# Laying out the model dimension as 512 a + 4 p + j in a two-layer trunk with a mixture of experts

## The chip, the cores and the metric

The kernel runs on one core of a Trainium2 chip. The metric is device time in microseconds (us), from the first to the last instruction of the program with what lies around them; lower is better. TensorE is called PE, its weight loads PEld, VectorE DVE, ScalarE ACT, GpSimd POOL and SyncE SP, as in the profile. MB is a million bytes, KB is 1024 bytes.

## What is computed

The reference is a trunk of two layers on 256 tokens of 1024 features, in 32-bit floats. Each layer has a mixer (layer 0: a convolution and a stick-breaking attention; layer 1: gated linear attention and pooling) and then a mixture of experts. The mixers are left out here; what the change is about is the second half of each layer, and it is mostly reading weights: 16 experts a layer with three matrices of 2 MB each.

```python
D_MODEL = 1024; SEQ = 256; DEPTH = 2; N_EXPERTS = 16; TOP_K = 2; D_EXPERT = 512
for l in range(DEPTH):
    mod = cond @ ada_w[l] + ada_b[l]                  # six vectors: shift, scale, gate, twice
    h = rmsnorm(x, norm_mix[l]) * (1 + sc1) + sh1
    x = x + g1 * mixer(h, w_in, w_out, ...)
    h = rmsnorm(x, norm_ffn[l]) * (1 + sc2) + sh2
    combine = weights of the two chosen experts of each token, zero elsewhere
    y = 0
    for e in range(N_EXPERTS):
        act = silu(h @ w_gate[l, e]) * (h @ w_up[l, e])      # 1024 -> 512
        y = y + combine[:, e] * (act @ w_down[l, e])         # 512 -> 1024
    x = x + g2 * y
return rmsnorm(x, final_norm)
```

## The kernel before, in words

**Layout.** A matrix with 1024 rows is used in eight blocks of 128 rows, one row on each partition. Which rows make a block is free, as long as the weights and the activations agree. `rows` (line 72) splits the row number as 256 a + 2 p + j, with a from 0 to 3, p the partition and j 0 or 1; block k is a = k // 2, j = k % 2, and `block` (line 76) picks it out of an array whose columns run over the features. In such a slice each element lies two elements behind the one before. It is read by PE as the matrix that is loaded into the array in the transposes of `vecs`, `xn` and `arow` (lines 129, 143, 197), in the output projection (line 451) and in the scatter of layer 0 (line 1323), and it is written as an output at line 1522.

**Units and the ring.** All large weights go through a ring of 16 buffers of 1 MB (8 KB a partition), `buffer` at line 50. A buffer's worth is called a unit here. Units are taken from the ring in the order in which the code asks for them, nearly all are loaded by DMAs that SP issues in that order, and a DMA waits on SP until the unit that lay in its buffer 16 units earlier has been read by its last matmul. `unit` (line 62) loads the projections' and the modulation's weights: `ada` with n = 2 (line 183) takes one row of 2048 columns on each partition, 8 KB in one piece; `Projections.load` (line 396) takes four rows of 512 columns, 2 KB each, in two DMAs.

**The experts.** They are worked off in eight pairs (`pr`), each expert with at most 64 tokens in the common case. `weight(pr, i)` (line 1206) loads unit i of a pair: 0 to 3 are `w_gate`, 4 to 7 `w_up`, 8 to 11 `w_down`. A unit holds a quarter of the rows of both experts of the pair: for `w_gate` and `w_up` the blocks 2i and 2i + 1, for `w_down` one block of 128 rows. On each partition that is 4 KB of one expert and 4 KB of the other. `up` (line 1231) takes a unit for every two blocks, and for each block one matmul of 512 columns for each expert; in the trace each such matmul is two instructions, so a unit is eight of them. `down` (line 1266) takes a unit for every block and does two halves of 512 columns for each expert. In names of tiles `w0_1_6` is layer 0, pair 1, unit 6; in the page the numbers are left out.

**Order.** The program is written out in its order by hand (`manual_schedule`). In layer 0, `up` of pair 0 has the gathers of the tokens between its blocks (`gathered`, line 1448, one gather of two blocks of `xg` for every two blocks of the matmul). From pair 1 on the order is gate, up, scatter of an earlier pair, down of the pair before, transposes of the activations. In pair 7 PE does the gate product, a scatter, a branch that skips code for experts with more than 64 tokens (`rest`, line 1369), the down product of pair 6, the up product of pair 7 in two halves with scatters, and the last down product. The mixers' projections take units of the same ring (`part`, line 398, splits a block of a unit into a high and a low half on ACT and DVE).

Of the kernel before, what the change touches and what calls it, by code (L numbers as in the profile page):

```python
# [16 lines left out]
D = 1024  # L17
# [12 lines left out]
def trunk(ctx: ExitStack, tc: tile.TileContext, x, c, ada_w, ada_b, norm_mix, norm_ffn,  # L30
# [31 lines left out]
    def unit(name, src, a, eng=SP):  # L62

        t = buffer(name).rearrange("p (a b) -> p a b", a=a)
        if len(src.shape) == 4:
            for i in range(2):
                eng.dma_start(t[:, 2 * i:2 * i + 2], src[:, i])
        else:
            eng.dma_start(t, src)
        return t  # L70

    def rows(w):

        return w.rearrange("(a p j) n -> p a j n", a=4, j=2)

    def block(ap, k):

        a, j = k // 2, k % 2
        return ap[:, 256 * a + j:256 * a + 256:2]
# [96 lines left out]
    def ada(l, s, n):  # L176
# [4 lines left out]
        for i in range(4 * n):  # L181
            if n == 2:
                w = unit(f"ad{nm_}{i}", src[:, i // 2, i % 2:i % 2 + 1, s * D:(s + 2) * D], 1)
            else:
                w = unit(f"ad{nm_}{i}", src[:, i, :, s * D:(s + 1) * D], 2)
# [44 lines left out]
    def small_loads():  # L230
        G.dma_start(rb, router_bias.rearrange("(o e) -> o e", o=1).broadcast_to([128, E]))
        for a in range(4):
            G.dma_start(rw[:, 2 * a:2 * a + 2], rows(router_w)[:, a])
        for a in range(4):
            G.dma_start(walow[:, 2 * a:2 * a + 2, 0:16], rows(w_in_odd[0])[:, a, :, 1536:1552])
# [151 lines left out]
    class Projections:  # L387
# [5 lines left out]
        def load(self, eng=SP):  # L393
            n, k = len(self.w) // 2, len(self.w) % 2 * 4
            c0 = self.firsts[n]
            self.w.append(unit(f"wi{c0}{k}", self.src[:, k // 2:k // 2 + 2, :, c0:c0 + 512], 4, eng))
# [723 lines left out]
    def moe(l, pool, nrm, psacc, after, following=None):  # L1120
# [85 lines left out]
        def weight(pr, i, out=None, eng=SP):  # L1206

            if i < 8:
                src = (moe_w_gate, moe_w_up)[i // 4][l, 2 * pr:2 * pr + 2]
                src = src.rearrange("e (a p j) n -> p a e (j n)", a=4, j=2)[:, i % 4]  # L1210
            else:
                src = moe_w_down[l, 2 * pr:2 * pr + 2, (i - 8) * 128:(i - 7) * 128].rearrange("e p n -> p e n")
            if out is None:
                out = buffer(f"w{l}_{pr}_{i}")
            if l and pr == 7 and i >= 10:

                out = out.rearrange("p (k e n) -> p k e n", k=2, e=2)
                for n in (last_parts[:1], last_parts[1:])[i - 10]:
                    for k in range(2):
                        src = moe_w_down[l, 14:16, (2 + k) * 128:(3 + k) * 128, n].rearrange("e p n -> p e n")  # L1220
                        SP.dma_start(out[:, k, :, within(n)], src)
                return out
            out = out.rearrange("p (e n) -> p e n", e=2)
            eng.dma_start(out, src)
            return out

# [4 lines left out]
        def up(pr, s, w, xg, name, between=None):  # L1231
            b = bank(f"{name}{l}_{pr}_{s}")
            o = 128 * (pr % 2)
            for k in range(8):
                if between:
                    between(k)
                if k % 2 == 0:
                    we = next(w)
                for e in range(2):
                    PE.matmul(b[64 * e:64 * e + 64, :], lhsT=xg[:, k, o + 64 * e:o + 64 * e + 64],  # L1240
                              rhs=we[:, e, k % 2 * 512:k % 2 * 512 + 512], start=k == 0, stop=k == 7)
            return b

        def act(pr, s, gb_, ub, sg=None):
# [8 lines left out]
            return a  # L1253
# [398 lines left out]
```

## Time and profile before

| | us |
|---|---|
| three runs: median (lowest, highest) | 797.86 (795.85, 861.59) |
| the profiled execution's own time | 801.36 |
| its span, first to last instruction | 799.6 |

The rows quoted below come from the profiled execution, all times in them from the start of its span. In a timeline a row gives the start, the time, the engine, the line, the operation, output and inputs, shapes and the count; a bracket at its end says how long the engine had been idle and what ended that. In the table by windows each engine's busy time is followed by its number of instructions, then come the granted PE clock (1.00 is 2.4 GHz), the mean busy share of the DMA engines and the rate in GB/s. A row "A <- B: t, n, m" of the waits says that A waited t us for B in n waits, the longest m.

### The profile page before, as it was taken

The numbers are of one execution on the slowest core, as the hardware profiler recorded it, in microseconds if no ns is written. First come the engines' busy times: TensorE is split into PE (matmuls) and PEld (weight loads), VectorE is DVE, ScalarE is ACT, GpSimd is POOL, SyncE is SP. The second block draws the span as 40 slices with busy tenths as digits, with TensorE's granted clock in tenths as the row PEclk, the third lists the DMA queues.
The fourth block names the chain that finished last, engine by engine and source line by source line (L and its number), as shares of the span: only waits on it lengthen the run. The fifth ranks groups of instructions, "written<-read, shape, count | busy, mean of one in ns | idle before, by whom it ended". The sixth has DMA issues, their size and how long they took to land. (4 is left out here: it accounts for less than half of the span.)

```text
span 799.6 us, 10666 instructions
## 1 busy us (share of the span) xinstructions
PE 736.6 (92%) x4177; PEld 404.3 (51%) x4177; DVE 314.4 (39%) x563; ACT 235.1 (29%) x441; POOL 118.9 (15%) x168
## 2 busy tenths in 40 slices
PE   7898798998999999999697999999699999999985
PEld 4498555586434344353233677578434334434323
DVE  4459968575213112130115655453513123213114
ACT  3357647463102001110113543551402001001012
POOL 2347646222000000000014500010200000000000
PEclk9999989999999999999989999999899999999988
DMA  9999739954999999999999997495799999999991
GB/s 358 385 376 419 267 120 394 372 224 192 351 412 409 409 409 409 410 408 409 407 401 389 401 413 247 182 390 204 292 362 411 410 409 409 410 410 409 408 381 58
DMA packets 74718, 282.52 MB, mean 353 GB/s; under 512 B 5194, under 2 KB 6438, under 8 KB 69530
## 3 DMA queue, kind: packets, MB, share of 16 engines
q1 hardware_dynamic: 73122, 278.68, 89.0%
q0 software_dynamic: 1344, 2.64, 0.9%
q8 instruction: 37, 0.61, 0.3%
q10 hardware_dynamic: 184, 0.34, 0.1%
q14 instruction: 31, 0.25, 0.1%
HBM read 280.59 MB, written 1.05 MB: 352 GB/s over the span
## 5 line engine op out<-in xcount | busy, mean ns | idle before, releaser
L1240 PE MATMUL g<-w,xg 128*64 128x512 f32 x512 | 115.9, 601 | 1.9 <-DMA w<-in_moe_w_gate_dram 1.8
L1273 PE MATMUL dn<-w,at 128*64 128x512 f32 x448 | 105.6, 623 | 11.5 <-PEq L1372 5.7
L1240 PE MATMUL u<-w,xg 128*64 128x512 f32 x496 | 110.6, 594 | 1.9 <-DMA w<-in_moe_w_up_dram 1.9
L1273 PEld LDWEIGHTS dn<-w,at 128*64 128x64 f32 x448 | 32.3, 143 | 77.0 <-issue 59.9
L1252 DVE TENSOR_TENSOR act<-sg,u 128x512 f32<-128x512 f32 (+1 forms) x18 | 11.1, 628 | 152.6 <-PE u L1240 152.6
L1240 PEld LDWEIGHTS u<-w,xg 128*64 128x64 f32 x496 | 34.7, 137 | 71.6 <-issue 64.7
L1240 PEld LDWEIGHTS g<-w,xg 128*64 128x64 f32 x512 | 35.3, 138 | 69.4 <-issue 62.9
L421 PE MATMUL pj<-hT,g 128*128 128x256 f32 x480 | 62.5, 288 | 7.0 <-DVE g L56 4.6
L56 DVE TENSOR_TENSOR g<-wi,g 128x512 fp32r<-128x512 f32 x72 | 58.2, 816 | 25.6 <-ACT g L55 24.5
L421 PEld LDWEIGHTS pj<-hT,g 128*128 128x128 f32 x480 | 59.2, 193 | 10.7 <-DVE g L56 6.7
L416 PE MATMUL pj<-g,hT 128*128 128x512 f32 x192 | 51.2, 414 | 7.5 <-DVE g L56 3.6
L55 ACT ACTIVATE g<-wi 128x512 fp32r<-128x512 f32 x72 | 44.4, 626 | 39.7 <-PE pj L421 20.9
L451 PE MATMUL po<-cat,g 128*128 128x256 f32 x372 | 51.1, 290 | 2.5 <-ACT gsr L994 1.7
L188 PE MATMUL ada<-ad,cond 128*32 128x512 f32 x384 | 50.6, 632 | 0.0
L451 PEld LDWEIGHTS po<-cat,g 128*128 128x128 f32 x372 | 46.8, 196 | 6.7 <-ACT gsr L994 2.6
L416 PEld LDWEIGHTS pj<-g,hT 128*128 128x128 f32 x192 | 35.6, 194 | 22.3 <-DVE g L56 6.7
L556 POOL TENSOR_TENSOR yc<-yc,cv 128x256 f32<-128x256 f32 x45 | 38.7, 860 | 24.3 <-ACT cv L555 21.6
L541 DVE SCALAR_TENSOR_TENSOR yc<-yp,epar,yc 128x256 f32<-128x256 f32 x56 | 41.2, 736 | 1.0
L1305 ACT ACTIVATE ys<-y 128x512 fp32r<-128x512 f32 x28 | 16.9, 625 | 70.4 <-DVE y L1295 50.2
L1263 DVE COPY at<-at 128x512 f32<-128x512 f32 x14 | 9.7, 692 | 68.0 <-PE at L1262 68.0
L1299 ACT ACTIVATE y<-dn,cw 128x512 f32<-128x512 f32 x7 | 4.8, 687 | 107.4 <-PE dn L1273 107.4
L1248 ACT ACTIVATE sg<-g 128x512 f32<-128x512 f32 x14 | 8.4, 597 | 89.4 <-PE g L1240 86.3
(385 smaller groups left out, 886.4 us busy)
## 6 DMA issues: line engine op xcount, KB each, us to landing
w<-in_moe_w_gate_dram SPq DMA_DIRECT2D x64, 1024.0 KB, 16.1
w<-in_moe_w_up_dram SPq DMA_DIRECT2D x62, 1024.0 KB, 18.4
w<-in_moe_w_down_dram SPq DMA_DIRECT2D x61, 1024.0 KB, 18.2
ad<-in_ada_w_dram SPq DMA_DIRECT2D x48, 1024.0 KB, 8.9
wi<-in_w_in_even_dram SPq DMA_DIRECT2D x20, 512.0 KB, 13.0
wi<-in_w_in_odd_dram SPq DMA_DIRECT2D x14, 512.0 KB, 12.6
wo<-in_w_out_even_dram SPq DMA_DIRECT2D x4, 1024.0 KB
wo<-in_w_out_odd_dram SPq DMA_DIRECT2D x4, 1024.0 KB, 16.6
```

The costliest lines, as they stand in the source:

```text
L55: S.activation(g[0], w, AF.Copy)
L56: (eng or V).tensor_tensor(g[1], w, g[0].bitcast(F32), op=OP.subtract)
L188: PE.matmul(acc[32 * j:32 * j + 32, :], lhsT=cond[:, k, :], rhs=w[:, k - (i if n == 2 else 2 * i), c0:c0 + 512], start=i == 0, stop=i == 4 ...
L416: PE.matmul(bs[t], lhsT=self.h[j][:, k, t * 128:(t + 1) * 128], rhs=g[i], start=k == 0 and p == 0, stop=k == 7 and p == 2)
L421: PE.matmul(bs[c // 2][:, (c % 2) * T:(c % 2 + 1) * T], lhsT=g[i][:, c * 128:(c + 1) * 128], rhs=self.h[j][:, k, :], start=k == 0 and c % ...
L451: PE.matmul(self.acc[kd // 2][:, (kd % 2) * T:(kd % 2 + 1) * T], lhsT=block(g[wi], kd % 4), rhs=cats[ci][:, k, :], start=start and kd % 2 ...
L541: V.scalar_tensor_tensor(yc[:, k], yp[:, k, j:j + T], epar[:, k, j:j + 1], yc[:, k], op0=OP.mult, op1=OP.add)
L556: G.tensor_tensor(y, y, p, op=OP.add)
L1240: PE.matmul(b[64 * e:64 * e + 64, :], lhsT=xg[:, k, o + 64 * e:o + 64 * e + 64], rhs=we[:, e, k % 2 * 512:k % 2 * 512 + 512], start=k == 0 ...
L1252: V.tensor_tensor(a[:, n], sg[:, n], ub[:, n], op=OP.mult)
L1273: PE.matmul(bs[h][64 * e:64 * e + 64, :], lhsT=at[k][:, 64 * e:64 * e + 64], rhs=r[:, e], start=k == 0, stop=k == 3)
L1305: S.activation(ys[:, 0, n], y[h], AF.Copy)
```

## The change

The row number is split as 512 a + 4 p + j, with a 0 or 1 and j from 0 to 3, so block k is a = k // 4, j = k % 4, and a slice of `block` has its elements four apart. A unit of an expert pair holds half the rows of one expert instead of a quarter of both: 8 KB of one expert in one piece on each partition. Even units belong to the pair's first expert, odd ones to the second. `up` takes two units for every four blocks, `down` takes two for every two. `w_down` is split in the same manner (`rows_down`, 256 a + 2 p + j), and so the transposes of the activations pick every other column. The projections' units are loaded by one DMA instead of two, with pieces of 2 KB as before; router weights and the small gate weights by two DMAs instead of four. The last units of layer 1 keep their size and shape. Left out of the diff are the same edits in `rest`.

```diff
--- before.py
+++ after.py
@@ -62,21 +62,17 @@
     def unit(name, src, a, eng=SP):
 
         t = buffer(name).rearrange("p (a b) -> p a b", a=a)
-        if len(src.shape) == 4:
-            for i in range(2):
-                eng.dma_start(t[:, 2 * i:2 * i + 2], src[:, i])
-        else:
-            eng.dma_start(t, src)
+        eng.dma_start(t, src)
         return t
 
     def rows(w):
 
-        return w.rearrange("(a p j) n -> p a j n", a=4, j=2)
+        return w.rearrange("(a p j) n -> p a j n", a=2, j=4)
 
     def block(ap, k):
 
-        a, j = k // 2, k % 2
-        return ap[:, 256 * a + j:256 * a + 256:2]
+        a, j = k // 4, k % 4
+        return ap[:, 512 * a + j:512 * a + 512:4]
 
     def halves(tile2):
         return tile2.rearrange("p (j t) -> p j t", j=2)
@@ -180,9 +176,9 @@
         src = rows(ada_w[l])
         for i in range(4 * n):
             if n == 2:
-                w = unit(f"ad{nm_}{i}", src[:, i // 2, i % 2:i % 2 + 1, s * D:(s + 2) * D], 1)
+                w = unit(f"ad{nm_}{i}", src[:, i // 4, i % 4:i % 4 + 1, s * D:(s + 2) * D], 1)
             else:
-                w = unit(f"ad{nm_}{i}", src[:, i, :, s * D:(s + 1) * D], 2)
+                w = unit(f"ad{nm_}{i}", src[:, i // 2, i % 2 * 2:i % 2 * 2 + 2, s * D:(s + 1) * D], 2)
             for j in range(4):
                 k, c0 = (i, j * 512) if n == 2 else (2 * i + j // 2, j % 2 * 512)
                 PE.matmul(acc[32 * j:32 * j + 32, :], lhsT=cond[:, k, :],
@@ -229,10 +225,10 @@
 
     def small_loads():
         G.dma_start(rb, router_bias.rearrange("(o e) -> o e", o=1).broadcast_to([128, E]))
-        for a in range(4):
-            G.dma_start(rw[:, 2 * a:2 * a + 2], rows(router_w)[:, a])
-        for a in range(4):
-            G.dma_start(walow[:, 2 * a:2 * a + 2, 0:16], rows(w_in_odd[0])[:, a, :, 1536:1552])
+        for a in range(2):
+            G.dma_start(rw[:, 4 * a:4 * a + 4], rows(router_w)[:, a])
+        for a in range(2):
+            G.dma_start(walow[:, 4 * a:4 * a + 4, 0:16], rows(w_in_odd[0])[:, a, :, 1536:1552])
         for j in range(4):
             G.dma_start(gw[32 * j:32 * j + 16], gla_gate_w[0])
 
@@ -393,7 +389,7 @@
         def load(self, eng=SP):
             n, k = len(self.w) // 2, len(self.w) % 2 * 4
             c0 = self.firsts[n]
-            self.w.append(unit(f"wi{c0}{k}", self.src[:, k // 2:k // 2 + 2, :, c0:c0 + 512], 4, eng))
+            self.w.append(unit(f"wi{c0}{k}", self.src[:, k // 4, :, c0:c0 + 512], 4, eng))
 
         def part(self):
             i = len(self.parts)
@@ -1205,24 +1201,27 @@
 
         def weight(pr, i, out=None, eng=SP):
 
+            e = 2 * pr + i % 2
             if i < 8:
-                src = (moe_w_gate, moe_w_up)[i // 4][l, 2 * pr:2 * pr + 2]
-                src = src.rearrange("e (a p j) n -> p a e (j n)", a=4, j=2)[:, i % 4]
+                src = rows((moe_w_gate, moe_w_up)[i // 4][l, e])[:, i // 2 % 2]
             else:
-                src = moe_w_down[l, 2 * pr:2 * pr + 2, (i - 8) * 128:(i - 7) * 128].rearrange("e p n -> p e n")
+                src = rows_down(e)[:, (i - 8) // 2]
             if out is None:
                 out = buffer(f"w{l}_{pr}_{i}")
             if l and pr == 7 and i >= 10:
 
                 out = out.rearrange("p (k e n) -> p k e n", k=2, e=2)
                 for n in (last_parts[:1], last_parts[1:])[i - 10]:
-                    for k in range(2):
-                        src = moe_w_down[l, 14:16, (2 + k) * 128:(3 + k) * 128, n].rearrange("e p n -> p e n")
-                        SP.dma_start(out[:, k, :, within(n)], src)
+                    for e in range(2):
+                        SP.dma_start(out[:, :, e, within(n)], rows_down(14 + e)[:, 1, :, n])
                 return out
-            out = out.rearrange("p (e n) -> p e n", e=2)
+            out = out.rearrange("p (j n) -> p j n", j=src.shape[1])
             eng.dma_start(out, src)
             return out
+
+        def rows_down(e):
+
+            return moe_w_down[l, e].rearrange("(a p j) n -> p a j n", a=2, j=2)
 
         def weights(pr, first, last):
             for i in range(first, last):
@@ -1234,11 +1233,11 @@
             for k in range(8):
                 if between:
                     between(k)
-                if k % 2 == 0:
-                    we = next(w)
+                if k % 4 == 0:
+                    we = [next(w), next(w)]
                 for e in range(2):
                     PE.matmul(b[64 * e:64 * e + 64, :], lhsT=xg[:, k, o + 64 * e:o + 64 * e + 64],
-                              rhs=we[:, e, k % 2 * 512:k % 2 * 512 + 512], start=k == 0, stop=k == 7)
+                              rhs=we[e][:, k % 4], start=k == 0, stop=k == 7)
             return b
 
         def act(pr, s, gb_, ub, sg=None):
@@ -1250,7 +1249,7 @@
             sg, ub = (b.rearrange("s (k p) -> s k p", k=4) for b in (sg, ub))
             for n in [slice(0, 4)] if pr < 7 else [slice(0, 2), slice(2, 4)]:
                 V.tensor_tensor(a[:, n], sg[:, n], ub[:, n], op=OP.mult)
-            return a
+            return a.rearrange("s k p -> s (k p)")
 
         def actT(pr, s, a, *at):
             nm_ = f"{l}_{pr}_{s}"
@@ -1259,7 +1258,8 @@
             at = [t.rearrange("p (k s) -> p k s", k=4)[:, 0:n] for t in at]
             for i, b in enumerate(bs):
                 for k in range(n):
-                    PE.transpose(b[:, k, :], a[:, i * n + k, :], ident)
+                    f = i * n + k
+                    PE.transpose(b[:, k, :], a[:, f // 2 * 256 + f % 2:f // 2 * 256 + 256:2], ident)
                 V.tensor_copy(at[i], b)
             return [t[:, k, :] for t in at for k in range(n)]
 
@@ -1270,19 +1270,20 @@
 
             def product(h, k, r):
                 for e in range(2):
-                    PE.matmul(bs[h][64 * e:64 * e + 64, :], lhsT=at[k][:, 64 * e:64 * e + 64], rhs=r[:, e],
+                    PE.matmul(bs[h][64 * e:64 * e + 64, :], lhsT=at[k][:, 64 * e:64 * e + 64], rhs=r[e],
                               start=k == 0, stop=k == 3)
 
-            for k in range(2 if l and pr == 7 else 4):
-                we = next(w)
-                for h, n in enumerate(cols):
-                    product(h, k, we[:, :, n])
+            for a in range(1 if l and pr == 7 else 2):
+                we = [next(w), next(w)]
+                for j in range(2):
+                    for h, n in enumerate(cols):
+                        product(h, 2 * a + j, [w_[:, j, n] for w_ in we])
             if l and pr == 7:
                 for h, n in enumerate(cols):
                     if h < 2:
                         we = next(w)
                     for k in range(2):
-                        product(h, 2 + k, we[:, k, :, within(n)])
+                        product(h, 2 + k, [we[:, k, e, within(n)] for e in range(2)])
             return bs
 
         def weighted(pr, s, bs, cw):
...
```

**Where instructions move.** On PE, in the gate product of pair 0 of layer 0 (`g0_0_0` is its output, `acc02` the bank of a gather between), before:

```order
L1240 MATMUL g0_0_0_1944<-w0_0_0_1955,xg0_0_1924 64x512 x4
L1175 MATMUL acc02_1920<-P0_0_1922,hn0h_1825 128x256 x2
L1175 MATMUL acc02_1920<-P0_0_1922,hn0l_1826 128x256 x2
L1175 MATMUL acc02_1920<-P0_0_1922,hn0h_1825 128x256 x2
L1175 MATMUL acc02_1920<-P0_0_1922,hn0l_1826 128x256 x2
L1240 MATMUL g0_0_0_1944<-w0_0_1_1971,xg0_0_1924 64x512 x4
```

And the same place of the changed kernel:

```order
L1239 MATMUL g0_0_0_1930<-w0_0_0_1941,xg0_0_1910 64x512
L1239 MATMUL g0_0_0_1930<-w0_0_1_1943,xg0_0_1910 64x512
...
L1171 MATMUL acc02_1906<-P0_0_1908,hn0h_1811 128x256 x2
L1171 MATMUL acc02_1906<-P0_0_1908,hn0l_1812 128x256 x2
L1171 MATMUL acc02_1906<-P0_0_1908,hn0h_1811 128x256 x2
L1171 MATMUL acc02_1906<-P0_0_1908,hn0l_1812 128x256 x2
L1239 MATMUL g0_0_0_1930<-w0_0_0_1941,xg0_0_1910 64x512
L1239 MATMUL g0_0_0_1930<-w0_0_1_1943,xg0_0_1910 64x512
```

Unit `w0_0_0` had been read to its end ahead of that gather; now its last matmul, and with it the point from which its buffer is free, stands behind the gather, beside that of `w0_0_1`.

On SP, the DMAs that stand 16 units behind those two, before (`w0_1_6` takes the buffer of `w0_0_0`, `w0_1_7` that of `w0_0_1`):

```order
L1224 DMA w0_1_5_2098<-in_moe_w_up_dram 128x2x1024
L1224 DMA w0_1_6_2104<-in_moe_w_up_dram 128x2x1024
L1224 DMA w0_1_7_2110<-in_moe_w_up_dram 128x2x1024
L1224 DMA w0_0_8_2129<-in_moe_w_down_dram 128x2x1024
L1224 DMA w0_0_9_2135<-in_moe_w_down_dram 128x2x1024
```

And of the changed kernel:

```order
L1219 DMA w0_1_5_2080<-in_moe_w_up_dram 128x2048
L1219 DMA w0_1_6_2090<-in_moe_w_up_dram 128x2048
L1219 DMA w0_1_7_2092<-in_moe_w_up_dram 128x2048
L1219 DMA w0_0_8_2115<-in_moe_w_down_dram 128x2048
L1219 DMA w0_0_9_2117<-in_moe_w_down_dram 128x2048
```

The order of the units on SP is what it was; each is now one run of 2048 elements on a partition instead of two of 1024.

## Rows read from the trace of the kernel before

**Rows 1.** The page: DMA packets, and DMA issues (KB each, us to landing).

```profile
DMA packets 74718, 282.52 MB, mean 353 GB/s; under 512 B 5194, under 2 KB 6438, under 8 KB 69530
...
w<-in_moe_w_gate_dram SPq DMA_DIRECT2D x64, 1024.0 KB, 16.1
...
ad<-in_ada_w_dram SPq DMA_DIRECT2D x48, 1024.0 KB, 8.9
```

**Rows 2.** Table by windows: PE, PEld, DVE, ACT, POOL busy, clock, DMA share, GB/s.

```profile
10.00:22.00 12.00, 12.00 (x59) 4.61 (x57) 5.72 (x9) 3.64 (x6) 5.23 (x8) 1.00 1.01 426
28.00:44.00 16.00, 12.77 (x86) 11.02 (x86) 11.65 (x21) 9.77 (x18) 7.54 (x8) 0.89 1.05 387
56.00:74.00 18.00, 15.99 (x129) 15.17 (x128) 16.41 (x22) 11.84 (x24) 11.07 (x12) 1.00 1.01 419
...
220.00:380.00 160.00, 156.40 (x802) 65.53 (x798) 32.68 (x54) 19.42 (x33) 0.00 (x0) 1.00 1.03 409
600.00:760.00 160.00, 157.80 (x782) 68.01 (x778) 38.52 (x63) 19.67 (x34) 0.00 (x0) 1.00 1.03 409
```

**Rows 3.** Waits of PE's weight loads, 200 to 410 us: those on DMAs.

```profile
PEld u L1240 <- DMA w<-in_moe_w_up_dram: 6.0, 5, 1.5
PEld dn L1273 <- DMA w<-in_moe_w_down_dram: 5.9, 6, 1.5
...
PEld g L1240 <- DMA w<-in_moe_w_gate_dram: 4.4, 3, 1.5
```

**Rows 4.** Waits of PE's weight loads, 560 to 800 us: the longest on DMAs.

```profile
PEld u L1240 <- DMA w<-in_moe_w_gate_dram: 0.9, 3, 0.3
```

**Rows 5.** Timeline of the weight loads, 330 to 400 us: waits for units.

```profile
338.62 0.20 PEld L1240 LDWEIGHTS u<-w,xg 128*64 128x64 f32 x4 [1.50 <-DMA w<-in_moe_w_up_dram]
...
385.16 0.20 PEld L1240 LDWEIGHTS g<-w,xg 128*64 128x64 f32 x4 [1.41 <-DMA w<-in_moe_w_gate_dram]
...
390.28 0.20 PEld L1240 LDWEIGHTS g<-w,xg 128*64 128x64 f32 x4 [1.51 <-DMA w<-in_moe_w_gate_dram]
```

**Rows 6.** Timeline of PE: pair 7 of layer 0, then pairs 6 and 7 of layer 1.

```profile
392.15 2.21 PE L1323 MATMUL acc<-pt,ys 128*128 128x256 f32 x16
...
400.06 9.88 PE L1273 MATMUL dn<-w,at 128*64 128x512 f32 x32 [5.70 <-PEq L1372]
...
741.04 7.09 PE L1273 MATMUL dn<-w,at 128*64 128x512 f32 x32
...
748.64 7.09 PE L1240 MATMUL g<-w,xg 128*64 128x512 f32 x32
...
761.79 9.92 PE L1273 MATMUL dn<-w,at 128*64 128x512 f32 x32 [3.99 <-ACTq L1372]
```

**Rows 7.** Timelines of PE and SP about 206 us: gate product, issues of w0_1_6 and w0_1_7.

```profile
203.94 2.11 PE L1240 MATMUL g<-w,xg 128*64 128x512 f32 x8
...
207.13 1.94 PE L1240 MATMUL g<-w,xg 128*64 128x512 f32 x8
...
206.09 0.37 SPq L1224 DMA_DIRECT2D w<-in_moe_w_up_dram  x1
...
209.10 0.37 SPq L1224 DMA_DIRECT2D w<-in_moe_w_up_dram  x1
```

**Rows 8.** Timeline of ACT at the first projection.

```profile
29.89 0.62 ACT L55 ACTIVATE g<-wi 128x512 fp32r<-128x512 f32 x1
31.25 1.09 ACT L383 ACTIVATE hT<-hf,mod,gc 128x256 fp32r<-128x256 f32 x2 [0.73 <-DVE gc L365]
```

**Rows 9.** Groups by line, weight loads (busy us, mean ns); then timeline of PE about 550 us.

```profile
L421 PEld LDWEIGHTS pj<-hT,g 128*128 128x128 f32 x480 | 59.2, 193 | 10.7 <-DVE g L56 6.7 <-DVE hT L327 1.5 <-ACT hT L383 1.3
L451 PEld LDWEIGHTS po<-cat,g 128*128 128x128 f32 x372 | 46.8, 196 | 6.7 <-ACT gsr L994 2.6 <-issue 1.8 <-ACT g L55 1.6
...
549.19 0.96 PE L291 MATMUL lg<-rwg,xT 128*128 128x16 f32 x8
...
550.82 3.13 PE L451 MATMUL po<-cat,g 128*128 128x256 f32 x24
```

More of the change, by code (lines that the diff above doesn't have):

```diff
@@ L1386, in rest @@
                                         w = spare[:, piece % 4]
-                                        SP.dma_start(w, rows(src[l, 2 * pr + e])[:, k // 2, k % 2])
+                                        SP.dma_start(w, rows(src[l, 2 * pr + e])[:, k // 4, k % 4])
                                         PE.matmul(b[64 * e:64 * e + 64, :], lhsT=quad.xg[:, k, o + 64 * e:o + 64 * e + 64],
@@ L1399, in rest @@
                                         w = spare[:, piece % 4]
-                                        SP.dma_start(w, moe_w_down[l, 2 * pr + e, k * 128:(k + 1) * 128, h * 512:(h + 1) * 512])
+                                        SP.dma_start(w, rows_down(2 * pr + e)[:, k // 2, k % 2, h * 512:(h + 1) * 512])
                                         PE.matmul(b[64 * e:64 * e + 64, :], lhsT=at[k][:, 64 * e:64 * e + 64],
```

## The prediction

> **What bounds the kernel now.** I read the DMA part of the page first, then a table by windows, then who waits for whom in each of the two expert stages, and last the timelines at the places found. The packets say that pieces of 8 KB exist already: 74718 less 69530 are 5188 of at least 8 KB [rows 1], and the 40 modulation loads with one row of 2048 columns on each of 128 partitions make 5120 of them. So the trace has a rate for each size. Pieces of 2 KB run at 387 GB/s, the experts' pieces of 4 KB at 409 in both layers, with the DMA engines busy all the time, and stretches mostly of 8 KB at 419 and 426 [rows 2]. The reader should see two things there: the rate rises with the piece, and a busy share of 1.03 in both expert stages makes the wire look like the limit of both.
>
> It is the limit of only one. In layer 0 PE's weight loads wait for expert units 14 times, 16.3 us in all [rows 3], and the last of these waits come at a fixed step: from 385.16 to 390.28 are two units, 2.56 us each [rows 5], which is 1024 KB at 409 GB/s. The stage starts with a stock of units, PE eats it faster than the wire refills it, and from about 336 us on it waits for each unit. In layer 1 the longest sum is 0.9 us in three waits [rows 4]; the down product that begins at 741.04 runs its 32 instructions in 7.09 us and the next product of 7.09 us begins at 748.64, with nothing between them but the transposes. The 3.99 us ahead of 761.79 is the branch, not a unit [rows 6]. There PE itself is the bound: a unit is eight instructions, 7.09 / 32 x 8 = 1.77 us, and with gathers, scatters, transposes and the branch that uses up the time. Behind the last wait of layer 0 (390.28, the fourth gate unit of pair 7) the path is PE's again: scatter at 392.15, branch, down product at 400.06 [rows 6], and then the vector work of layer 1's mixer.
>
> **The change part by part.** I sum against the profiled execution, 801.36 us with a span of 799.6. It lies 3.5 us above the median of the three runs, 797.86; I apply the difference to the median.
>
> *Larger pieces.* A unit takes 1.0486 MB / 409 GB/s = 2.564 us now. At 419 to 426 it takes 2.503 to 2.461, so 0.06 to 0.10 are saved; I take 0.08, the middle, since both windows hold a few smaller pieces. What counts is the units between the last stall of the wire and the last wait of PE: from w0_1_6 (issued at 206.09 [rows 7]) to the fourth gate unit of pair 7 are 2 + 4 + 5 x 12 + 4 = 70. That is -5.6 us (-4.3 to -7.2) for the landing of that unit.
>
> *Buffers come free later.* At the start of layer 0's experts the ring is full. The first block pair of the gate product runs from 203.94 to about 206, SP issues w0_1_6 at 206.09; the second from 207.13 to about 209, and SP issues w0_1_7 at 209.10 [rows 7]. After the change both units are read to the end of the fourth block, so both DMAs are issued at about 209.1, the first 3.0 us late. As two units then go down the wire behind each other at 2.5 us, where they came 3.0 apart, the second is late by 2.5: +2.5 us on everything behind it (bounds 0, if the wire has other work at that time, and 3.0). Behind SP's wait only later units are queued. The buffers of the third and fourth unit also come free together, but that lies beside the two transfers ahead of them.
>
> *Pairs of units.* While PE waits for the wire it can start only when a unit of each expert is there, and then has sixteen instructions left instead of eight: 1.77 us more between the last landing and the end of the product. A little of it overlaps, since the first expert's first matmul can go ahead; +1.7 us (1.5 to 1.8). It is paid once, behind the last wait.
>
> *Projection units in one DMA.* ACT's first split at 29.89 needs half a unit of 2 KB pieces today; the other half comes 0.524 MB / 387 GB/s = 1.35 us later. ACT's split would end at 31.86 at the latest instead of 30.51, and its next work waits for DVE until 31.25 anyway [rows 8]: 0 to +0.6 us, I take 0.3. Fewer DMA issues on SP and POOL free time on queues that wait for others; 0.
>
> *Slices with a step of four.* 372 recorded weight loads in the output projections read such a slice, and so do the scatters of layer 0. The trace shows steps of one and two: 193 ns against 196 [rows 9]. A step of four it does not show. Below nothing there is no reason; above, a load could take twice as long (rival C). I take 0, the nearest row.
>
> *Layer 1's experts.* PE does not wait there, so a faster wire gives nothing, and at most 0.9 us of waits can go. The second unit of a pair is needed 1.77 us sooner than now, and the stall at the start of the stage grows as in layer 0; both are covered by units that lie ready and by the 0.08 us that the wire gains a unit, 5.0 us over the 62 units between 600 and 760 us. If that cover is too thin, some 2 us come back as waits. I take 0.
>
> Sum: -5.6 + 2.5 + 1.7 + 0.3 = -1.1 us: 800.3 in a profiled execution like this one, 796.8 as a median. The bounds of the terms alone give -5.7 (-7.2 + 1.5) to +1.1 (-4.3 + 3.0 + 1.8 + 0.6), and the runs shown differ by 2 us.
>
> **Rivals.** *A: the whole saving reaches the end.* If both expert stages were bound by the wire to their end, all 192 expert units would count: 192 x 0.08 = 15.4 us, 782.5 us. For it speak the busy share of 1.03 in both stages and the steady 409 GB/s [rows 2]; against it that PE in layer 1 hardly waits for a unit [rows 4, 6], and that a late start and the pairing take part of it back. The Trainium skill (Perfetto Trace Analysis, DMA Optimizations) says that going from 2 KB to 4 or 8 KB can raise throughput dramatically and is the first thing to do where a kernel is DMA-bound; by that rule one would expect this case. The trace agrees with its direction, 387, 409 and about 423 GB/s, but the last step is 3%.
>
> *B: 8 KB pieces bring nothing for the experts' matrices.* The faster windows read another matrix, beside other work. If the rate stays at 409, what is left is +3.0 + 1.8 + 0.6 = +5.4: 803.3 us, slower but within 2%. Against it: two windows of different stages agree within 2%.
>
> *C: the step of four slows the weight loads.* A product with 16 columns is paced by its weight load: eight in 0.96 us are 0.12 us each. The output projection's products of 256 columns come 24 in 3.13 us, 0.13 each [rows 9]: load and product are about equally long, and a longer load would show at once. If a load took twice its 0.12 us, each product would come 0.24 - 0.13 = 0.11 later: 0.11 x 372 = 41 us, and about 4 for some 40 scatters behind the last wait of layer 0. That gives 796.8 + 45 = 842 us. It decides as soon as a load takes more than 0.13 us. For it speaks that PE has no waiting time under these products. Against it: a step of two costs 3 ns, and a load takes 0.12 us for 128 columns where a product passes 256 columns in 0.13, so a load has twice the time for each element. The Trainium skill (SBUF - State Buffer, the note on cachelines under "Door 1") speaks for C: lines of 16 bytes, with at least two accesses to a line needed for full speed. A step of two 4-byte elements has two to a line, one of four has one; no run here shows the latter.
>
> **How the numbers follow.** Forecast 0.79, A 0.05, B 0.09, C 0.07. The forecast's own case lies within 792 and 800. The range goes down to 790 (797.86 - 5.7, less 2 us between runs) and up to 805 (B and 2 us); A and C lie outside with 0.12. Two per cent is 16 us, about what a measurement of this kernel tells from no change. A reaches it with the upper rate alone (0.10 a unit), so faster has 0.03; slower is C, 0.07; within 2% has the other 0.90.
>
> **What would show it right or wrong.** Right: 220 to 380 us at 418 to 426 GB/s; w0_1_6 and w0_1_7 issued together near 209; PE's waits in layer 0 in steps of about 5 us, two units each, and the gate product of pair 7 ending 1 to 2 us earlier; layer 1's products still 7.09 us with no waits for units; the weight loads of line 451 at 196 ns and its products 0.13 us apart. Wrong: a rate of 409 (B); products of line 451 0.15 us apart or more (C); layer 1's stage shorter by several us (A); or new waits for units in layer 1, which I cost at nothing.

## The result

The changed kernel takes 846.88 us (median of four runs, 846.68 to 850.66), the kernel before 798.20 (median of four): a ratio of 1.062 with a 95% interval of 1.0585 to 1.0653. It is slower by 48.7 us, and the forecast of 796.8 with its range to 805 was wrong; rival C, at 842, is what happened. The profiled execution took 846.78 us with a span of 845.0, 45.4 us more than the span before.

The table divides the spans at three places of PE's timeline: the first product of the ranking that opens layer 0's experts (`rk`, line 1092), the first norm sum behind these experts (`ss`, line 268), and the first `rk` of layer 1. The first and third stage hold a mixer each, the second and fourth the experts. E1 and E3 to E6 are experiments below.

| us | mixer 0 | experts 0 | mixer 1 | experts 1 and end |
|---|---|---|---|---|
| before | 199.2 | 231.0 | 136.0 | 233.5 |
| changed | 220.3 | 234.9 | 154.6 | 235.3 |
| E1, only the output projection's loads at step four | 220.2 | 229.4 | 156.7 | 231.7 |
| E3, only the scatter's loads at step four | 200.0 | 235.1 | 134.3 | 231.8 |
| E4, changed, output projection packed in blocks | 209.8 | 235.5 | 136.4 | 233.3 |
| E5, changed, both packed in pairs | 200.9 | 228.7 | 133.3 | 232.9 |
| E6, as E5, one expert after the other | 200.3 | 258.0 | 134.7 | 264.4 |

Stages differ by 1 to 3 us between kernels whose instructions there are alike. For experts 0, before and E1 are such a pair, 231.0 and 229.4 us; 1.1 us of that is the down product behind the branch, 9.88 us before [rows 6] and 8.76 in E1, with a granted clock of 0.72 and of 0.86 in the 10 us from its start. The other differences are not explained here. Most of the loss lies in the two mixers (+21.1 and +18.6 of the 45.4 us), which the prediction had left at +0.3.

**The profile after.** The groups by line, first those that answer to [rows 9] (line 447 was 451, line 417 was 421, line 1324 was 1323; busy us and mean ns of one):

```profile
L447 PEld LDWEIGHTS po<-cat,g 128*128 128x128 f32 x372 | 88.8, 330 | 5.0 <-ACT gsr L990 2.6 <-issue 1.3 <-ACT g L55 0.8
L417 PEld LDWEIGHTS pj<-hT,g 128*128 128x128 f32 x480 | 59.3, 193 | 10.6 <-DVE g L56 6.6 <-DVE hT L323 1.5 <-ACT hT L379 1.3
L1324 PEld LDWEIGHTS acc<-pt,ys 128*128 128x128 f32 x128 | 30.6, 328 | 7.8 <-issue 6.5 <-ACT ys L1316 0.8 <-DVE ys L1317 0.5
L193 PEld LDWEIGHTS acol<-ident,arow 128*128 128x128 f32 x28 | 3.9, 209 | 5.1 <-ACT arow L189 5.1
...
L447 PE MATMUL po<-cat,g 128*128 128x256 f32 x372 | 92.2, 405 | 1.7 <-ACT gsr L990 1.7
```

The timeline of PE, an output projection in mixer 0 and a scatter, against 3.13 us in [rows 9] and 2.21 in [rows 6]:

```profile
200.96 5.86 PE L447 MATMUL po<-cat,g 128*128 128x256 f32 x24
...
396.33 4.01 PE L1324 MATMUL acc<-pt,ys 128*128 128x256 f32 x16
```

A load from an array written by ACT and DVE takes 330 ns where its columns are four elements apart, and 196 where they are two apart. The loads of line 417, whose columns are neighbours, are unchanged. The products follow the load: 5.86 / 24 = 0.24 us each where 3.13 / 24 = 0.13 stood. Times 384 (372 and 12 in two small groups) the difference of 0.114 us is 44 us, and E1 below shows that nearly all of it reaches the end.

The DMA part came as predicted. Page and table by windows (the columns are those of [rows 1, 2]):

```profile
DMA packets 49983, 282.53 MB, mean 334 GB/s; under 512 B 4842, under 2 KB 5958, under 8 KB 20474
```

```profile
28.00:44.00 16.00, 12.81 (x86) 10.90 (x85) 11.59 (x21) 9.88 (x18) 7.40 (x7) 0.89 1.05 387
...
260.00:400.00 140.00, 140.00 (x690) 67.78 (x686) 31.06 (x50) 18.81 (x32) 0.00 (x0) 1.00 1.01 421
660.00:800.00 140.00, 140.00 (x704) 60.85 (x704) 34.72 (x55) 16.67 (x29) 0.00 (x0) 1.00 1.01 421
```

Both expert stages now run at 421 GB/s instead of 409 [rows 2]; the mixer's pieces of 2 KB stay at 387. But PE is busy in all 140 of 140 us of both windows. The waits of its weight loads for units, 200 to 460 us, where [rows 3] summed to 16.3 us:

```profile
PEld u L1239 <- DMA w<-in_moe_w_gate_dram: 0.3, 1, 0.3
```

The slower scatters have used up the time in which PE waited, so a faster wire has nothing left to give.

### The profile page after: what moved, and what is told of

It reads as the page before. It is cut to its first block, busy times and chain, and to the rows that moved or that the text cites. A ratio compares the mean times of both kernels' runs of the same rounds, so it can differ in the third digit from the quotient of the medians.

```text
span 845.0 us, 10614 instructions
## 1 busy us (share of the span) xinstructions
PE 794.5 (94%) x4177; PEld 467.4 (55%) x4177; DVE 313.6 (37%) x563; ACT 235.8 (28%) x441; POOL 116.9 (14%) x163
## 5 line engine op out<-in xcount | busy, mean ns | idle before, releaser
L1273 PE MATMUL dn<-w,at 128*64 128x512 f32 x448 | 103.5, 617 | 8.2 <-ACTq L1373 8.2
L447 PE MATMUL po<-cat,g 128*128 128x256 f32 x372 | 92.2, 405 | 1.7 <-ACT gsr L990 1.7
L447 PEld LDWEIGHTS po<-cat,g 128*128 128x128 f32 x372 | 88.8, 330 | 5.0 <-ACT gsr L990 2.6
L1324 PEld LDWEIGHTS acc<-pt,ys 128*128 128x128 f32 x128 | 30.6, 328 | 7.8 <-issue 6.5
```

Source lines behind the costliest of these rows:

```text
L447: PE.matmul(self.acc[kd // 2][:, (kd % 2) * T:(kd % 2 + 1) * T], lhsT=block(g[wi], kd % 4), rhs=cats[ci][:, k, :], start=start and kd % 2 ...
L1273: PE.matmul(bs[h][64 * e:64 * e + 64, :], lhsT=at[k][:, 64 * e:64 * e + 64], rhs=r[e], start=k == 0, stop=k == 3)
L1324: PE.matmul(acc[k // 2][:, (k % 2) * T:(k % 2 + 1) * T], lhsT=block(ys[i], k), rhs=pt, start=first and k % 2 == 0 and i == 0, stop=last an ...
```

## Experiments

### E1: the step alone, in the kernel before

```diff
-                PE.matmul(self.acc[kd // 2][:, (kd % 2) * T:(kd % 2 + 1) * T], lhsT=block(g[wi], kd % 4),
+                PE.matmul(self.acc[kd // 2][:, (kd % 2) * T:(kd % 2 + 1) * T], lhsT=g[wi][:, kd % 4:512:4],
```

> The kernel before with one edit: the weight loads of the output projections (line 451) take every fourth column of a block of 512 instead of every second of 256; other columns than the reference's are multiplied, the work is the same. Theory (the step of four slows the load, and the load paces the product): loads of line 451 about 330 ns instead of 196, 24 products in about 5.9 us instead of 3.13, so 372 x 0.11 = 41 us, nearly all on the path: 838 to 842 us, and both mixers about 20 us longer. Rival (the layout's other parts, larger pieces, pairs of units or one DMA a unit, cost the 49 us): loads stay at 196 ns and the time at 798.

Measured: 839.41 us, ratio 1.052 (1.048 to 1.056), with the old units, the old DMAs and the old order. Groups by line:

```profile
L451 PEld LDWEIGHTS po<-cat,g 128*128 128x128 f32 x372 | 88.7, 329 | 5.0 <-ACT gsr L994 2.6 <-issue 1.3 <-ACT g L55 0.8
L451 PE MATMUL po<-cat,g 128*128 128x256 f32 x372 | 92.1, 405 | 1.7 <-ACT gsr L994 1.7
```

These are the changed kernel's numbers, and mixer 0 and mixer 1 take what they take there, to 2 us. One slice expression makes 41.5 of the 48.7 us.

### E2: a step of three

```diff
-                PE.matmul(self.acc[kd // 2][:, (kd % 2) * T:(kd % 2 + 1) * T], lhsT=block(g[wi], kd % 4),
+                PE.matmul(self.acc[kd // 2][:, (kd % 2) * T:(kd % 2 + 1) * T], lhsT=g[wi][:, kd % 4:kd % 4 + 382:3],
```

> The kernel before with the same slices at a step of three (12 bytes); other columns are multiplied, the work is the same. If what counts is how many 16-byte lines a load touches (64 at a step of two, 96 at three, 128 at four), a load lies half way between 196 and 330 ns, 263, a product about 0.18 instead of 0.13 us apart, and the time is up by 372 x 0.05 = 19 us: about 817. If any step above two is slow, it is as with four: about 840. If only four is slow (a step that is a power of two, each element at the same place of its line), nothing changes: 798.

Measured: 1058.23 us, which none of the three expected. The total tells nothing of the loads: with other columns the tokens fell on other experts, some got more than 64, and the code that the branch otherwise skips ran (192 products of line 1388 and 1401, which the kernel before doesn't execute). The loads can be read by themselves; groups by line, then PE's timeline:

```profile
L451 PEld LDWEIGHTS po<-cat,g 128*128 128x128 f32 x372 | 67.2, 263 | 5.1 <-ACT gsr L994 2.6 <-issue 1.7 <-ACT g L55 0.8
...
L1388 PE MATMUL o<-spare,xg 128*64 128x512 f32 x128 | 58.8, 658 | 28.4 <-DMA spare<-in_moe_w_gate_dram 22.7 <-DMA spare<-in_moe_w_up_dram 5.4
```

```profile
179.15 4.55 PE L451 MATMUL po<-cat,g 128*128 128x256 f32 x24
```

263 ns is just half way between 196 and 330, and a product comes every 4.55 / 24 = 0.19 us. The start of layer 0's experts is at 209.28, 10.1 us later than before, half of E1's 21.0. So it is no cliff between two and four.

### E3: the step in the scatter alone

```diff
-                        PE.matmul(acc[k // 2][:, (k % 2) * T:(k % 2 + 1) * T], lhsT=block(ys[i], k),
+                        PE.matmul(acc[k // 2][:, (k % 2) * T:(k % 2 + 1) * T], lhsT=ys[i][:, 512 * (k // 4) + k % 4:512 * (k // 4) + 512:4],
```

> The kernel before with only the scatters of layer 0 (line 1323) at a step of four; other columns are multiplied, the work is the same. Theory: 16 products in 4.0 instead of 2.2 us, 14 us of PE in eight pairs. Most of it takes the place of the 16.3 us in which PE waits for units; behind the last such wait lie two to three scatters, so the end moves by 4 to 6 us: 802 to 804. Rival (the expert stage cannot hide it): the whole 14 us, 812. If only the output projection's loads are slow: 798.

Measured: 803.65 us, ratio 1.008 (1.005 to 1.010): +5.7 us. The 128 loads take 328 ns each, and PE's products of this line 32.6 us instead of 18.1; group of E3:

```profile
L1323 PE MATMUL acc<-pt,ys 128*128 128x256 f32 x128 | 32.6, 406 | 0.3 <-DVE ys L1316 0.3
```

Part of these 14.5 us goes where PE had been idle. Before, PE itself waited 5.4 us for units in layer 0; the 16.3 us of [rows 3], which my expectation took for PE's, are waits of its loads, which run ahead of the products. PE's own waits of before:

```profile
PE u L1240 <- DMA w<-in_moe_w_up_dram: 1.9, 3, 0.6
PE g L1240 <- DMA w<-in_moe_w_gate_dram: 1.8, 3, 0.6
PE dn L1273 <- DMA w<-in_moe_w_down_dram: 1.7, 3, 0.7
```

In E3 these are gone. The only wait of a load for a unit that is left in layer 0, and the down product behind the branch on PE's timeline:

```profile
PEld dn L1273 <- DMA w<-in_moe_w_up_dram: 0.3, 1, 0.3
```

```profile
402.18 9.63 PE L1273 MATMUL dn<-w,at 128*64 128x512 f32 x32 [4.01 <-PEq L1372]
```

Counted from the `rk` product, pair 7's gate product ends 1.2 us later than before (+194.25 against +193.05), with 80 of the 128 products ahead of that point. Of the 48 behind it, the first 16 take 1.8 us longer, but the wait at the branch that follows is shorter by nearly as much (4.01 us instead of 5.70 [rows 6]); the other 32 cost 3.6 us. So 803.65 lies in my range of 802 to 804 partly by luck: the scatter ahead of the branch, which I counted in, costs almost nothing.

The stage takes 235.1 us here with the old units and 234.9 in the changed kernel with the new ones: with slow scatters no gain of the larger pieces can be read.

### E7: a step of eight

```diff
-                        PE.matmul(acc[k // 2][:, (k % 2) * T:(k % 2 + 1) * T], lhsT=block(ys[i], k),
+                        PE.matmul(acc[k // 2][:, (k % 2) * T:(k % 2 + 1) * T], lhsT=block(ys[i], k) if last else ys[i][:, k:1024:8],
```

> The kernel before with the scatters of layer 0 (but the last pair's) at a step of eight, other columns, the same work. The loads took 196, 263 and 330 ns at steps of two, three and four. If what counts is how many 16-byte lines are touched (64, 96, 128), a step of eight touches 128 too: about 328 ns, 16 products in 4.0 us. If it is the distance that a load passes over (67 ns for each element of the step), 596 ns, and 16 products in 8.3 us.

Measured: one run, 803.28 us. Groups by line, 260 to 400 us, where all scatters have the step of eight:

```profile
L1323 PEld LDWEIGHTS acc<-pt,ys 128*128 128x128 f32 x96 | 23.7, 338 | 4.9 <-issue 4.9
```

338 ns and not 596: the load does not pay for the distance. Steps of 1, 2, 3, 4 and 8 took 193, 196, 263, 328 to 330 and 338 ns, which follows the number of 16-byte lines that 128 elements touch (32, 64, 96, 128, 128) with a floor at 64. The Trainium skill (SBUF - State Buffer, the note on cachelines under "Door 1") names such lines and at least two accesses to each for full speed, and these loads agree with that. The same note puts the step that is free at "4 fp32"; with that they do not agree, as a step of three already costs 67 ns. That lines are the cause, and not some other unit with the same counts, was not measured apart; and the loads of the transposes of plain floats do not follow this count (last section).

### E4 and E8: neighbours for PE, the step for ACT and DVE

```diff
-                self.g[n][k, q] = split(buffers(i), ws[k // 2][:, k % 2, 512 * q:512 * q + 512], G if i in pool else None)
+                w = ws[k // 2][:, k % 2, 512 * q:512 * q + 512].rearrange("p (m j) -> p j m", j=4)
+                g = self.g[n][k, q] = buffers(i)
+                split([t.rearrange("p (j m) -> p j m", j=4) for t in g], w, G if i in pool else None)
...
-                PE.matmul(self.acc[kd // 2][:, (kd % 2) * T:(kd % 2 + 1) * T], lhsT=block(g[wi], kd % 4),
+                PE.matmul(self.acc[kd // 2][:, (kd % 2) * T:(kd % 2 + 1) * T], lhsT=g[wi][:, kd % 4 * 128:kd % 4 * 128 + 128],
```

E8 has the same places with "p m j" on both sides: neighbours are read, and written 128 elements apart.

> The changed kernel with one edit: ACT and DVE write the high and low halves of the output projection's weights block by block, so that PE's loads there read neighbouring elements, while ACT and DVE read with a step of four. Theory: the loads of line 447 fall from 330 to about 195 ns, 24 products from 5.9 to 3.1 us, and 41 us are given back: 806 us (803 to 809, as ACT's and DVE's reading with a step may cost something). Rival (other parts of the layout cost the time): at most a few us back, above 840.

> The changed kernel with the output projection's copies packed into four blocks as in the run that packed them before, but ACT and DVE go through them the other way: they read neighbours and write with a distance of 128 elements. If reading with a step of four was what doubled ACT's copies (0.62 to 1.12 us), they are back near 0.62 us and the time is about 10 us below that run, 805. If writing with a distance costs as much: 1.1 us a copy and 815 again.

Measured: E4 814.82 us, ratio 1.021 (1.017 to 1.024); E8 816.6 in one run. Some 32 of the 41 us come back. PE's loads are down to 202 ns in E4, and ACT's copies have grown. Groups by line and shape of before, of E4 and of E8:

```profile
L55 ACT ACTIVATE g<-wo 128x512 fp32r<-128x512 f32 x31 | 18.4, 621 | 1.5 <-PE po L451 1.5
```

```profile
L55 ACT ACTIVATE g<-wo 128x512 fp32r<-128x512 f32 x31 | 34.1, 1131 | 1.4 <-PE po L449 1.3
```

```profile
L55 ACT ACTIVATE g<-wo 128x512 fp32r<-128x512 f32 x31 | 33.0, 1129 | 1.5 <-PE po L449 1.5
```

The price has moved from PE's read to ACT's and DVE's (DVE's copies take 1111 and 1133 ns instead of 774), and ACT's is the same whether the read or the write is the one with the distance. In mixer 1 that hides (136.4 us, as before), in mixer 0 PE waits for the copies; PE's timeline of E4:

```profile
163.12 1.45 PE L449 MATMUL po<-cat,g 128*128 128x256 f32 x10 [0.57 <-DVE g L56]
166.64 0.51 PE L449 MATMUL po<-cat,g 128*128 128x256 f32 x2 [2.07 <-ACT g L55]
```

My expectation of 806 (803 to 809) gave the copies' step 3 us at most, with no row that showed it: the same mistake as in the prediction.

### E5: two elements of each line for everyone

The copies keep neighbours in pairs, so nobody touches a line for one element only: ACT and DVE read and write pairs, PE loads with a step of two. The scatter's input is written in the same manner, straight from PSUM.

```diff
+    def pairs(ap, k):
+        a, j = k // 2, k % 2
+        return ap[:, 256 * a + j:256 * a + 256:2]
...
+                w = ws[k // 2][:, k % 2, 512 * q:512 * q + 512].rearrange("p (m a j) -> p a m j", a=2, j=2)
+                g = self.g[n][k, q] = buffers(i)
+                split([t.rearrange("p (a m j) -> p a m j", a=2, j=2) for t in g], w, G if i in pool else None)
...
-                PE.matmul(self.acc[kd // 2][:, (kd % 2) * T:(kd % 2 + 1) * T], lhsT=block(g[wi], kd % 4),
+                PE.matmul(self.acc[kd // 2][:, (kd % 2) * T:(kd % 2 + 1) * T], lhsT=pairs(g[wi], kd % 4),
...
-                        PE.matmul(acc[k // 2][:, (k % 2) * T:(k % 2 + 1) * T], lhsT=block(ys[i], k),
+                        PE.matmul(acc[k // 2][:, (k % 2) * T:(k % 2 + 1) * T], lhsT=pairs(ys[i], k),
```

> The changed kernel, but the copies that PE loads are written in two groups of 256 columns, neighbours kept in pairs: PE loads them with a step of two, as before the change, in the output projections and in the scatters of layer 0, and ACT and DVE read and write pairs of 8 bytes. Theory: the loads are back at 196 ns, and ACT's copies, which took 1.12 us when they read with a step of four, are back at 0.62, since a pair of a line is read at once. Then what is left of the change is the layout and its DMAs, for which the terms of the prediction stand: layer 0's experts 229.6 us instead of 231.0 (-5.6 + 2.5 + 1.7), all in all 797 (793 to 800). Rival 1 (any packing costs ACT its half microsecond a copy): 805 to 808, with layer 0's mixer 10 us longer. Rival 2 (the layout costs something else too): loads at 196 and copies at 0.62, but a time above 803.

Measured: 797.44 us, ratio 0.998 (0.9951 to 1.0004). Groups by line:

```profile
L453 PEld LDWEIGHTS po<-cat,g 128*128 128x128 f32 x372 | 46.8, 196 | 7.2 <-ACT gsr L996 2.7 <-issue 1.8 <-ACT g L55 1.7
L1338 PEld LDWEIGHTS acc<-pt,ys 128*128 128x128 f32 x128 | 16.1, 195 | 7.6 <-issue 6.5 <-ACT ys L1329 0.8 <-DVE ys L1331 0.3
...
L55 ACT ACTIVATE g<-wo 128x512 fp32r<-128x512 f32 x31 | 19.9, 669 | 1.4 <-PE po L453 1.2
```

The loads are back, a copy costs 48 ns more than before, and the whole loss of 48.7 us is gone with the layout, the pieces of 8 KB and the pairs of units still in place. So neither of these costs anything that can be measured. The kernel now also lets the other terms of the prediction be read, which slow loads hide in the changed kernel; timelines of SP, of PE's loads and of PE:

```profile
210.88 0.80 SPq L1225 DMA_DIRECT2D w<-in_moe_w_up_dram  x2
...
383.57 0.33 PEld L1245 LDWEIGHTS g<-w,xg 128*64 128x64 f32 x4 [0.53 <-DMA w<-in_moe_w_gate_dram]
388.54 0.20 PEld L1245 LDWEIGHTS g<-w,xg 128*64 128x64 f32 x4 [2.07 <-DMA w<-in_moe_w_gate_dram]
...
392.12 2.21 PE L1338 MATMUL acc<-pt,ys 128*128 128x256 f32 x16
```

### E6: one expert after the other

```diff
-            for k in range(8):
...
-                if k % 4 == 0:
-                    we = [next(w), next(w)]
-                for e in range(2):
+            for k, e in [(4 * a + j, e) for a in range(2) for e in range(2) for j in range(4)]:
...
+                if k % 4 == 0:
+                    we = next(w)
```

> As the kernel of the two groups of 256 columns, and the expert products take a unit's four blocks (of the down product its two) for one expert before they begin the other unit, instead of going back and forth between two units. PE can then start when one unit is there, and a unit's buffer is free after its own eight products. If the prediction's terms for the pairs (+1.7) and for buffers that come free later (+2.5) were real, 2 to 4 us go: about 794. If these terms were nothing, the time is that of the other kernel, within 1 us.

Measured: 859.68 us, ratio 1.075 (1.071 to 1.079), far from the 794 and the 797 of my expectation. The waits for units are gone, but the gate products take 147.6 us in place of 115.7 in E5. The group of E6, and the timeline of its loads at the start of a product:

```profile
L1244 PE MATMUL g<-w,xg 128*64 128x512 f32 x512 | 147.6, 599 | 0.0
```

```profile
222.54 0.14 PEld L1244 LDWEIGHTS u<-w,xg 128*64 128x64 f32 x1 [0.29 <-issue]
222.97 0.14 PEld L1244 LDWEIGHTS u<-w,xg 128*64 128x64 f32 x1 [0.29 <-issue]
223.40 0.14 PEld L1244 LDWEIGHTS u<-w,xg 128*64 128x64 f32 x1 [0.29 <-issue]
223.83 0.19 PEld L1244 LDWEIGHTS u<-w,xg 128*64 128x64 f32 x3 [0.29 <-issue]
```

Every 0.43 us one load is issued here until the second expert's instructions come up, then two or three. In the kernel before it is two at each step, as in this row of its loads:

```profile
600.63 0.14 PEld L1240 LDWEIGHTS u<-w,xg 128*64 128x64 f32 x2 [0.29 <-issue]
```

The two experts of a pair use the two halves of PE's columns, and their products run side by side. Without a partner some steps of 0.43 us are half empty in each product; the up products grow as much as the gate products (143.7 us for 111.5), the down products by 22.7 us. (The Trainium skill, TensorE: Matmul & The Clock Gate, Part 3, says that matmuls in different column tiles run at the same time; the trace agrees, with two loads every 0.43 us before and one where the partner is missing.) What the edit was meant to win cannot be read behind that loss.

### E9 and E10: the scatter into the wait

```diff
-            gb_ = up(pr, 0, w, quad.xg, "g", None if pr else gathered)
+            gb_ = up(pr, 0, w, quad.xg, "g", {0: gathered, 7: None if l else both_halves}.get(pr))
```

`both_halves` issues the scatter of pair 7 ahead of the fifth block, and its old place is left out; E9 on E5, E10 on the kernel before.

> The kernel with the copies in pairs (two groups of 256 columns), and in layer 0's pair 7 the scatter that stood behind the gate product now stands between its fourth and fifth block, where PE waits 2.07 us for the last two units (PE had them at 388.54 and the scatter ended at 394.3). The scatter needs no unit and takes 2.21 us, so it fits into that wait: if the last landing sets the end of layer 0, 2 us go: 795.4. Rival (the branch behind, 5.67 us, takes up what is won, or the scatter's input is late): 797.4 as without the edit.

> The kernel before with the same scatter between the fourth and fifth block of pair 7's gate product. The waits of the gate product's last two units (0.62 and 0.63 us on PE) lie behind that place; the fourth block ends at about 387.1, the scatter would run to 389.3, the third unit is then there and the fourth (390.28) when the third is done at 391.2. So the scatter and product end at 393.1 instead of 394.3: 1 us less, 797. The same rivals: 798.

Measured: 798.50 us, ratio 1.001 (0.9987 to 1.0032), and 797.12, ratio 1.000 (0.9972 to 1.0024). E9's interval excludes the 2 us of its theory. (They came from the 2.07 us that PE's loads wait; PE itself is idle for 1.19 us there.) E10's total cannot tell 797 from 798; its timeline can. PE's timeline of E10, the gate product's second half and the row that answers to the 5.70 us in [rows 6]:

```profile
389.62 3.99 PE L1240 MATMUL g<-w,xg 128*64 128x512 f32 x16
...
400.73 1.97 PE L1273 MATMUL dn<-w,at 128*64 128x512 f32 x4 [7.11 <-ACTq L1372]
```

From the `rk` product, gate product and scatter are both done at +193.7 in E10 (393.61 - 199.89) and at +195.2 before (394.36 - 199.18), but the down product begins at 200.8 us (400.73 - 199.89) and at 200.9 (400.06 - 199.18): the branch gives back what the scatter had won. ACT's queue is now named as what PE waits for, where PE's own sequencer was named before. From the end of the gate product to the down product are 7.8 us before, with the scatter between them, and 7.1 us in E10 without it. So all but some 0.7 of the scatter's 2.2 us lay beside that chain already; that the chain starts with ACT's reading of the gate product is argued, not shown. No kernel here is measurably faster than the one before.

## Why the prediction was wrong

**The step that failed** is *Slices with a step of four*: "I take 0, the nearest row." Its two ends were 0 and 41 us, and I took the lower one because the rows for steps one and two, 193 and 196 ns, were 3 ns apart. That is no trend when the quantity that counts has a floor at two elements to a line. E1 puts this term at 41.5 us; it was the upper bound of the prediction's own working, 0.11 x 372.

**Rival C** was right in its mechanism and close in size: 842 us against 846.9. Its two arguments against were wrong. "A step of two costs 3 ns" says nothing of four, and that a load "has twice the time for each element" didn't help it. Its rate of two was a little high for the load (330 / 196 = 1.68), and right for the spacing (0.24 us). The 0.12 us that it calls a load is a spacing too: recorded loads of 196, 263 and 330 ns came 0.13, 0.19 and 0.24 us apart (before, E2, changed). The "about 4" for scatters behind the last wait is 5.7 in E3, and not by that path alone (E3 above). With a chance of 0.07 and a range that ended at 805, the price of 41 us on an operation that no row showed was left out of the range.

The sum now: 41.5 (E1) and 5.7 (E3) are 47.2 of 48.7 us, and the interval of the ratio is 2.7 us wide to each side. In E5 the other edits bring experts 0 down by 2.3 us against before and by 0.7 against E1, which has the old units too; with the slow scatters no gain can be read.

**The other terms**, read in E5 against before, each from the `rk` product (200.94 and 199.18):

- *Larger pieces* and *buffers come free later*: w0_1_6 and w0_1_7 are issued together, at +9.94 instead of +6.91 and +9.92 [rows 7]; the first is 3.0 us late, as worked out. The last gate unit of pair 7 is there at +187.60 instead of +191.10: -3.5, where -5.6 + 2.5 = -3.1 was said. (In E1, with the old units, it is there at +190.63: -3.0.) The two terms are not told apart by this.
- *Pairs of units*: waits come 4.97 us apart (383.57, 388.54), two units each. From the last landing to the scatter are 3.58 us instead of 1.87 [rows 5, 6]: +1.7, as said; the gate product ends 1.8 us earlier than before.
- *Projection units in one DMA*: in the changed kernel ACT's first split begins at 30.61 instead of 29.89, and its next work at 31.38 instead of 31.25 [rows 8]. E1 with the old loads has 31.41 there, so nothing of the +0.3 is to be seen.
- *Layer 1's experts*: 0.7 us of waits for units (1.2 before) and products of 7.09 us, as before; nothing won or lost can be read.

Forecast without the slices, and E5, are 796.8 and 797.4; E5 has slightly longer copies besides. That the totals meet so closely is partly luck: a sum of -1.1 us cannot be told from nothing by E5's interval, and it is the timelines above that bear the terms out. **Rival A** fell: at 421 GB/s in both stages no 15 us appear. **Rival B** fell with the rate. The path behind the last wait held one misreading: the scatter at 392.15 counted as part of it, and E10 shows that all but some 0.7 us of it runs beside the branch's chain.

## What to carry to other kernels

A layout that makes DMA pieces longer also fixes the step at which PE, ACT and DVE read the same data, and the step is the term to price first: here a rate 3% higher in the expert stages was worth 1 to 2 us in one stage, which the total does not show, and the step cost 47. Where a layout forces four elements apart, let the copy that is made anyway keep pairs of neighbours together, so that each reader takes two elements of every 16 bytes (E5); a full transposition into blocks moves the price to the copy, which hid in one mixer here and cost some 10 us in the other (E4, E8). Where no row shows an operation and its bounds lie 41 us apart, the range has to hold both.

## What the runs showed that was not expected

- Weight loads of arrays written as fp32r, at steps of 1, 2, 3, 4 and 8 elements of 4 bytes: 193, 196, 263, 328 to 330 and 338 ns.
- The transposes of `arow`, whose 32-bit floats are not written as fp32r, went from a step of two to four without a change: 208 and 209 ns a load. The same change took the transposes of the activations, plain floats as well, from a step of one to two, and there the load did get longer, from 140 to 207 ns (rows of before and of the changed kernel, below). So in these loads the price seems to come at a step of two, and four adds nothing; why stays open, and no run tried it.

```profile
L1262 PEld LDWEIGHTS at<-ident,act 128*128 128x128 f32 x64 | 6.9, 140 | 11.2 <-issue 10.8 <-PE acc L1429 0.2
```

```profile
L1262 PEld LDWEIGHTS at<-ident,act 128*128 128x128 f32 x64 | 9.0, 207 | 11.1 <-issue 10.8 <-PE acc L1430 0.2
```

- A write with a distance costs ACT as much as a read with one: 1131 and 1129 ns a copy of 512 elements, against 621, and 669 in pairs.
- Two experts' products in the two halves of PE's columns run side by side; putting one expert's products behind the other's cost 62 us (E6).
